# A streaming-encoder layer on one core: another issue order in the opening, residual rows loaded ahead, outputs finished in place, two divided weight units placed elsewhere

## The chip, the core and the metric

The kernel runs on one core of a Trainium2 chip. The metric is the device time of one execution in microseconds. The core has five engines that each work through their own instructions in order: TensorE (PE, matrix products and transposes; PEld is its weight load), VectorE (DVE), ScalarE (ACT), GpSimd (POOL) and SyncE (SP). Transfers between memory and the core's SBUF are issued by an engine and run on 16 DMA engines. Nearly all are issued by SP here, a few by POOL. An issue stands in its engine's order like any other instruction.

## The reference

The input is `x`, 2048 frames of 1024 float32 values. One layer is computed (DEPTH is 1):

```
h    = rmsnorm(x, norm_mix)
proj = h @ w_in                        # 1024 -> 2560 columns for four groups
y_a = short gated convolution          # columns cv_h, cv_b, cv_c
y_b = S5 state-space scan + GLU        # s5_u, with log_dt, lam, b, c, d
y_c = sliding-window attention         # a_q, a_k, a_v
y_d = HGRN2 gated linear recurrence    # hg_q, hg_f, hg_i, hg_g
y = rmsnorm of each group, concatenated
x = x + y @ w_out
h = rmsnorm(x, norm_ffn)
x = x + square(relu(h @ w_ff1)) @ w_ff2
```

## The kernel before

Frames lie in four blocks of 512 (`NB`, `TB`). Every matrix product is done in a split form: each float32 operand becomes a high and a low part, and a product takes three matmuls (hi·hi, lo·hi, hi·lo). At the clock's full level one 128x512 matmul follows the next every 0.23 us.

**The opening.** `make_hT(b)` loads the four 128-frame tiles of a block (`xt`, two buffers), squares each on ACT (L486), forms the mean on DVE (`rsx`, L92) and its power -1/2 on POOL (L93), scales on DVE with the gain row `g_mix` (L488), transposes on PE (L501), and copies the transposed halves out as `hh` (ACT, L505) and `hl` (DVE, L506). `attn_in` then multiplies tile by tile with the attention columns of `w_in`; `load_split` loads each weight tile `wr` through SP and splits it into `wh` (ACT, L105) and `wl` (DVE, L111). Behind it stand the HGRN columns, whose first matmul of the swapped kind is `mm<-hh,wh`. Some 15 small constants are loaded through POOL (`mraw` to `wgr`, L146 to L199), and then those of the S5 set-up (`lam`, `cn`, `bn`, `ldt`, `db`, L229 to L244). The two `ldt` loads are gathers of single 4-byte elements. A tile scheduler decides the order on each engine from the order of the program text and from priorities (`first`, `tc.high_priority`).

**The output projection.** `outp(b)` makes for each half `nh` of the columns four row tiles `i`; `ps` is the product in PSUM, `xr` the residual rows of `x` (two buffers), their sum goes to DRAM as `x1d`.

**The second feed-forward product.** It runs as seven groups `n` = 0 to 6 of eight row tiles `q` (a Strassen form); each tile is 16 units of three matmuls (L1548). `s_tile` loads and splits the moving side (`sr`, `st`), `t_unit` the weight units of the next group; `split2` puts the split units in turn into 26 slots. `X` and `Y` are running sums in SBUF. `finish` ends a row tile of the output:

```
r = tmp2(); SY.dma_start(out=r, in_=x1_d[...])
tsub(r, r, acc, ALU.add)        # acc is X or Y: tq<-tq,X
o = tmp2(); tsub(o, ps, r, ALU.add)   # tq<-mm,tq
SY.dma_start(out=a["out"][...], in_=o)
```

It is called for n = 1, 5 and twice for n = 6. `psum_mm` has two buffers, so a product that is not yet read holds back the one after the next.

Of the kernel before, what the change touches and what calls it, by code (L numbers as in the profile page):

```python
# [59 lines left out]
def emit(ctx, tc, a):  # L60
# [150 lines left out]
    def s5_setup():  # L211
        with tc.tile_pool(name="st", bufs=1) as st:
# [256 lines left out]
            for gp in range(8):  # L469
# [6 lines left out]
                yield  # L476


    def make_hT(b):

        def norm(i):
            t0 = b * TB + i * P
            xt = big.tile([P, D], F32, tag="xt", name="xt", bufs=2)
            SY.dma_start(out=xt, in_=a["x"][t0:t0 + P, :])
            ss = mix.tile([P, 1], F32, tag="ssx", name="ssx", bufs=2)
            S.activation(out=junk, in_=xt, func=AF.Square, accum_out=ss)  # L486
            r = rstd_of(mix, ss, 1, 1.0 / D, "rsx")
            V.scalar_tensor_tensor(out=xt, in0=xt, scalar=r, in1=g_mix, op0=ALU.mult, op1=ALU.mult)  # L488
            return xt

        nx = norm(0)
        yield
        for i in range(4):
            xt = nx
            if i < 3:
                nx = norm(i + 1)
            for k4 in range(2):
                pt = psum_tr()
                for k in range(4):
                    kk = k4 * 4 + k  # L500
                    PE.transpose(pt[:, k * P:(k + 1) * P], xt[:, kk * P:(kk + 1) * P], ident)  # L501
                pv = pt.rearrange("p (k t) -> p k t", k=4)
                oh = hh[:, k4 * 4:k4 * 4 + 4, i * P:(i + 1) * P]
                ol = hl[:, k4 * 4:k4 * 4 + 4, i * P:(i + 1) * P]
# [1088 lines left out]
```

## Time and profile before

| | |
|---|---|
| median of 3 runs | 2293.39 us (2293.31 to 2297.61) |
| profiled execution, its own time | 2296.33 us |
| its span, first to last instruction | 2294.5 us |
| mean granted clock | 0.992 |
| PE busy | 2205.3 us, 96% |
| DVE / ACT / POOL busy | 63% / 42% / 8% |
| DMA | 372.97 MB, mean 163 GB/s |

The span is what the trace shows; the execution's own time has 1.8 us around it. Times of instructions below count from the start of the span. In a row of the timeline stand start, duration, engine and line, operation, what it writes and reads, and in brackets how long the engine was idle just before and what it waited for.

### The profile page before, as it was taken

To read this page: it belongs to the slowest core of one execution; us is meant where nothing else is said; L and a number is where in the kernel's file an instruction comes from. 1 tells how busy PE (TensorE), PEld (TensorE's weight loads), DVE (VectorE), ACT (ScalarE), POOL (GpSimd) and SP (SyncE) were. 2 spreads that over 40 slices of the span, in tenths; PEclk is the share of its full clock that TensorE was granted. 3 is DMA by queue.
4 is the path that set the end of the run, shared out by engine and by line. 5 is a ranking of instruction groups with operands and counts; after the bars stand their busy time and mean duration, and the time that the engine had idled before them with its cause. 6 is when DMAs were issued, how large, how long until landed. Compare 5 with 4: busy or idle time off the path is not lost.

```text
span 2294.5 us, 32511 instructions
## 1 busy us (share of the span) xinstructions
PE 2205.3 (96%) x11460; PEld 1755.9 (77%) x11460; DVE 1449.5 (63%) x3044; ACT 961.3 (42%) x1914; POOL 194.4 (8%) x251
## 2 busy tenths in 40 slices
PE   4999999999999999999999999999999999999899
PEld 3777777777777787777788878888878877888787
DVE  4796796797679664596666676555534455465343
ACT  3444325324433433465565565555533223223121
POOL 3112212112211210000000000000000010000000
PEclk9999999999999999999999999999999999999999
DMA  6333334333443457646667575554655587475544
GB/s 174 97 89 94 98 98 138 109 105 100 139 116 104 129 195 232 196 153 202 195 196 210 151 235 156 152 148 147 201 165 195 181 293 233 146 248 175 190 165 152
DMA packets 391476, 372.97 MB, mean 163 GB/s; under 512 B 30656, under 2 KB 305184, under 8 KB 391312
## 3 DMA queue, kind: packets, MB, share of 16 engines
q1 hardware_dynamic: 388976, 365.05, 51.7%
q0 software_dynamic: 2336, 5.84, 1.0%
q8 instruction: 90, 1.47, 0.3%
q14 instruction: 74, 0.61, 0.1%
HBM read 265.97 MB, written 103.82 MB: 161 GB/s over the span
## 4 chain that ended last, share of the span: by engine, by line
PE 42%; DMA 6%; DVE 3%; ACT 1%; issue 1%; SPq 0%; DVEq 0%; ACTq 0%
PE mm L1548 19%; PE mm L1363 13%; PE hx L1363 7%; DMA wr<-in_w_ff_dram 5%; PE mx L1363 3%; DVE st L1520 1%; DMA tr<-tb 1%; DMA sr<-as 1%; DVE wr L1217 1%; DVE wl L1208 0%; ACT wh L1207 0%; ACT st L1519 0%; DMA tq<-x1d 0%; DVE tp L1217 0%; DVE tb L1327 0%
## 5 line engine op out<-in xcount | busy, mean ns | idle before, releaser
L1548 PE MATMUL mm<-wh,st 128*128 128x512 f32 x1728 | 549.2, 395 | 13.8 <-DVE tq L1217 6.1
L1548 PEld LDWEIGHTS mm<-wh,st 128*128 128x128 f32 x1728 | 325.8, 189 | 92.3 <-issue 9.6
L1548 PE MATMUL mm<-wl,st 128*128 128x512 f32 x864 | 341.1, 395 | 0.2 <-DVE wl L1208 0.2
L1363 PE MATMUL mm<-tb,wh 128*128 128x512 f32 x1024 | 323.8, 397 | 4.0 <-ACT tp L1369 1.9
L1519 ACT ACTIVATE st<-sr 128x1024 fp32r<-128x1024 f32 x112 | 115.4, 1054 | 343.6 <-PE mm L1548 244.2
L1363 PEld LDWEIGHTS mm<-tb,wh 128*128 128x128 f32 x1024 | 190.9, 189 | 53.7 <-ACT tp L1382 5.4
L510 PE MATMUL mm<-wh,hh 128*128 128x512 f32 x512 | 212.4, 415 | 0.7 <-ACT hh L505 0.7
L512 PE MATMUL mm<-wh,hl 128*128 128x512 f32 x512 | 205.9, 402 | 0.0
L105 ACT ACTIVATE wh<-wr 128x512 fp32r<-128x512 f32 x224 | 138.2, 629 | 158.6 <-PE mm L511 113.8
L511 PE MATMUL mm<-wl,hh 128*128 128x512 f32 x512 | 204.6, 400 | 0.0
L1363 PE MATMUL mm<-tb,wl 128*128 128x512 f32 x512 | 202.4, 396 | 1.0 <-DVE wl L1208 1.0
L1207 ACT ACTIVATE wh<-wr 128x512 fp32r<-128x512 f32 x204 | 124.8, 627 | 176.1 <-DVE wr L1217 83.4
L1548 PEld LDWEIGHTS mm<-wl,st 128*128 128x128 f32 x864 | 162.8, 188 | 38.9 <-DVE wl L1208 0.9
L1520 DVE TENSOR_TENSOR st<-sr,st 128x1024 fp32r<-128x1024 f32 x112 | 134.5, 1221 | 70.6 <-ACT st L1519 70.5
L111 DVE TENSOR_TENSOR wl<-wr,wh 128x512 fp32r<-128x512 f32 x224 | 150.2, 690 | 35.8 <-ACT wh L105 34.7
L1363 PE MATMUL hx<-tb,wh 128*128 128x512 f32 x512 | 161.1, 394 | 0.0
L1208 DVE TENSOR_TENSOR wl<-wr,wh 128x512 fp32r<-128x512 f32 x204 | 136.6, 687 | 36.5 <-ACT wh L1207 30.2
L510 PE MATMUL mm<-hh,wh 128*128 128x512 f32 x384 | 159.4, 415 | 0.0
L512 PE MATMUL mm<-hh,wl 128*128 128x512 f32 x384 | 152.7, 398 | 0.0
L511 PE MATMUL mm<-hl,wh 128*128 128x512 f32 x384 | 152.3, 397 | 0.0
L1363 PEld LDWEIGHTS mm<-tb,wl 128*128 128x128 f32 x512 | 96.6, 189 | 23.7 <-DVE wl L1208 1.4
L510 PEld LDWEIGHTS mm<-wh,hh 128*128 128x128 f32 x512 | 98.6, 193 | 20.8 <-ACT hh L505 1.3
(412 smaller groups left out, 3617.1 us busy)
## 6 DMA issues: line engine op xcount, KB each, us to landing
wr<-in_w_ff_dram SPq DMA_DIRECT2D x304, 256.0 KB, 3.9
as<-tp SPq DMA_DIRECT2D x224, 256.0 KB, 2.7
sr<-as SPq DMA_DIRECT2D x112, 512.0 KB, 4.6
wr<-in_w_in_dram SPq DMA_DIRECT2D x160, 256.0 KB, 3.1
wr<-in_w_out_dram SPq DMA_DIRECT2D x64, 256.0 KB, 4.0
xt<-in_x_dram SPq DMA_DIRECT2D x16, 512.0 KB, 3.6
xr<-in_x_dram SPq DMA_DIRECT2D x32, 256.0 KB, 3.0
x1d<-xr SPq DMA_DIRECT2D x32, 256.0 KB, 2.5
```

The source lines that it names most:

```text
L105: S.activation(out=hi, in_=raw, func=AF.Copy)
L111: (G if le == "p" else V).tensor_tensor(out=lo, in0=raw, in1=hi, op=ALU.subtract)
L510: PE.matmul(ps, lhsT=lh, rhs=rh, start=first, stop=False)
L511: PE.matmul(ps, lhsT=lh, rhs=rl, start=False, stop=False)
L512: PE.matmul(ps, lhsT=ll, rhs=rh, start=False, stop=last)
L1207: S.activation(out=h, in_=raw, func=AF.Copy)
L1208: V.tensor_tensor(out=l, in0=raw, in1=h, op=ALU.subtract)
L1217: V.tensor_tensor(out=o, in0=x, in1=y, op=op)
L1363: PE.matmul(ps, lhsT=(wh, wl)[lw][:, ks], rhs=b[lb][:, k, :], start=first and k == 0 and q == 0, stop=k == 3 and q == 2, skip_group_check= ...
L1519: S.activation(out=s_[:, 0, ks], in_=r, func=AF.Copy)
L1520: V.tensor_tensor(out=s_[:, 1, ks], in0=r, in1=s_[:, 0, ks], op=ALU.subtract)
L1548: PE.matmul(ps, lhsT=st_[:, ls, k, :], rhs=tu[n, k][lt], start=k == 0 and p_ == 0, stop=k == NJ - 1 and p_ == 2)
```

## The change

1. `make_hT` and its first run stand ahead of the constants in the program text. All constants are issued behind the first power on POOL (`tc.issue_after(norms[0][0])`), the loads of the S5 set-up behind the fourth, and the first part of block 0's `attn_in` behind the first scaling. `issue_after` orders instructions that are on the same engine; it adds no wait between engines.
2. `outp` issues the load of `xr` ahead of the row tile's matmuls, with high priority.
3. In the second feed-forward product `ahead(n, q)` loads the residual rows and adds X or Y to them in the turn of the tile before; `finish(ps, rs)` then adds `ps` in place and stores.
4. In `split2` the 10th and 11th unit go to the slots in pool `c1` ("xr", "gain"), which were the 25th and 26th; the others keep the slots in `t2p`.

```diff
-        G.tensor_tensor(out=r, in0=r, in1=mhalf[:, 0:n], op=ALU.pow)
+        pows.append(G.tensor_tensor(out=r, in0=r, in1=mhalf[:, 0:n], op=ALU.pow).ins)
...
+    with first(-4000):
+        run(make_hT(0))
+    after = tc.issue_after(norms[0][0])
+    after.__enter__()
     masks = cm.tile([P, 4, P], U8, name="masks")
     mraw = mix.tile([P, 4, P], F32, tag="cva0", name="mraw")
     G.dma_start(out=mraw, in_=a["c_masks"])
...
+    after.__exit__(None, None, None)
...
-                ps = yield from tm_tile(ws, i)
                 xr = c1.tile([P, 512], F32, tag="xr", name="xr", bufs=2)
                 t0 = b * TB + i * P
-                SY.dma_start(out=xr, in_=a["x"][t0:t0 + P, ns])
+                with tc.high_priority():
+                    SY.dma_start(out=xr, in_=a["x"][t0:t0 + P, ns])
+                ps = yield from tm_tile(ws, i)
...
-    next(setup)
+    with tc.issue_after(norms[3][0]):
+        next(setup)
     for b in range(NB):
-        dense(attn_in(b))
+        g = attn_in(b)
+        if b == 0:
+            with tc.issue_after(norms[0][1]):
+                next(g)
+        dense(g)
...
-        if n < NW + NB2:
+        if n == NW:
+            return split(raw, c1, ("xr", "xr"), 2)
+        if n > NW + 1:
             return split(raw, t2p, ("vh", "vl"), NB2)
-        if n == NW + NB2:
-            return split(raw, c1, ("xr", "xr"), 2)
...
+    ENDS = {1: (("X", 0, 0),), 5: (("X", 1, 0),), 6: (("X", 1, 1), ("Y", 0, 1))}
+    def ahead(n, q):
+        t0, rs = (q % 4) * P, []
+        for acc, tb, nd in ENDS.get(n, ()):
+            b_ = (q // 4) * 2 + tb
+            r = tmp2()
+            SY.dma_start(out=r, in_=x1_d[b_][t0:t0 + P, nd * 512:(nd + 1) * 512])
+            tsub(r, r, (X if acc == "X" else Y)[:, q], ALU.add)
+            rs.append((r, a["out"][b_ * TB + t0:b_ * TB + t0 + P, nd * 512:(nd + 1) * 512]))
+        return rs
+    def finish(ps, rs):
+        for r, dst in rs:
+            tsub(r, ps, r, ALU.add)
+            SY.dma_start(out=dst, in_=r)
...
             if (n, q) != (6, 7):
                 s_next = s_tile(*((n, q + 1) if q < 7 else (n + 1, 0)))
+                r_next = ahead(*((n, q + 1) if q < 7 else (n + 1, 0)))
...
-            elif n == 5:
-                finish(q, ps, X[:, q], 1, 0)
-            else:
-                finish(q, ps, X[:, q], 1, 1)
-                finish(q, ps, Y[:, q], 0, 1)
+            finish(ps, ends)
```

The first place where instructions move is the opening, on DVE and on POOL. On DVE, of before, from its first conversion to the first `hl`:

```order
L147 CAST masks<-mraw 128x512
L92 TENSOR_SCALAR rsx<-ssx 128x1
L111 TENSOR_TENSOR wl<-wr,wh 128x512 x7
L488 SCALAR_TENSOR_TENSOR xt<-xt,rsx,g_mix 128x1024
L111 TENSOR_TENSOR wl<-wr,wh 128x512
```

The same stretch of the changed kernel, whose line numbers differ:

```order
L94 TENSOR_SCALAR rsx<-ssx 128x1
L168 SCALAR_TENSOR_TENSOR xt<-xt,rsx,g_mix 128x1024
L94 TENSOR_SCALAR rsx<-ssx 128x1
L113 TENSOR_TENSOR wl<-wr,wh 128x512 x2
L168 SCALAR_TENSOR_TENSOR xt<-xt,rsx,g_mix 128x1024
L187 TENSOR_TENSOR hl<-tr,hh 128x4x128
L113 TENSOR_TENSOR wl<-wr,wh 128x512 x3
```

The scaling of the first tile stood behind the mask conversion and seven weight splits, and stands behind none now. Further on in DVE's order is the first operation that reads `ldt`, of before with the fourth `hl` of the opening's eight ahead of it:

```order
L506 TENSOR_TENSOR hl<-tr,hh 128x4x128
L742 COPY va<-mm 128x128
L223 TENSOR_SCALAR t_783<-ldt 128x8
L217 TENSOR_TENSOR db<-db,ident 16x256
L766 TENSOR_REDUCE qss<-qsq 128x6
```

and of the changed kernel, with all eight `hl` ahead of it:

```order
L187 TENSOR_TENSOR hl<-tr,hh 128x4x128
L793 TENSOR_TENSOR qn<-qk,qrs 128x128
L168 SCALAR_TENSOR_TENSOR xt<-xt,rsx,g_mix 128x1024
L273 TENSOR_SCALAR t_783<-ldt 128x8
L267 TENSOR_TENSOR db<-db,ident 16x256
L271 TENSOR_SCALAR t_784<-t_783 128x8
L271 TENSOR_SCALAR t_784<-t_784 128x8
L761 COPY va<-mm 128x128
```

The operation on `ldt` now stands behind the whole of the opening's own work on DVE and ahead of the copy `va<-mm` of a later `attn_in` tile.

On POOL, of before, the loads up to the first power (`rsx<-rsx,mhalf`):

```order
L146 DMA mraw<-in_c_masks_dram 128x512
L149 DMA bones<-in_c_bones_dram 128x2
L154 DMA g_grp<-in_group_norm_dram 128x768
L156 DMA g_grpa<-in_group_norm_dram 128x2x1
L159 DMA convw<-in_conv_w_dram 128x3x1 x2
L165 DMA qgain<-in_attn_q_norm_dram 64x1 x2
L165 DMA kgain<-in_attn_k_norm_dram 64x1 x2
L168 DMA sink<-in_attn_sinks_dram 64x2x1
L93 ISA
L93 TENSOR_TENSOR rsx<-rsx,mhalf 128x1
```

and of the changed kernel, its first six rows of work:

```order
L95 ISA
L95 TENSOR_TENSOR rsx<-rsx,mhalf 128x1
L198 DMA mraw<-in_c_masks_dram 128x512
L201 DMA bones<-in_c_bones_dram 128x2
L203 DMA g_grp<-in_group_norm_dram 128x768
L95 TENSOR_TENSOR rsx<-rsx,mhalf 128x1
```

The first power stood behind eleven loads and stands ahead of all now. The S5 set-up loads, which stood behind the second power, come later in the changed kernel, behind the third and fourth:

```order
L223 DMA ogain<-in_hg_out_norm_dram 128x64
L226 DMA lbp<-in_hg_lower_bounds_dram 128x2x1
L248 DMA wgr<-in_s_w_glu_dram 128x512 x2
L95 TENSOR_TENSOR rsx<-rsx,mhalf 128x1 x2
L279 DMA lam<-in_s_lam_re_dram 8x128
L280 DMA lam<-in_s_lam_im_dram 8x128
```

The eleven set-up loads follow one another from `lam` on, with `ldt` and `db` last, as they did.

The second place is SP in the output projection of block 1, where its second half of columns begins (`x1d<-xr` is the store of a finished row tile, `ybt` the loads of the next stage). Of before:

```order
L1109 DMA xr<-in_x_dram 128x512
L1112 DMA x1d_64<-xr 128x512
L102 DMA wr<-in_w_out_dram 128x512 x8
L1112 DMA x1d_64<-xr 128x512
L1109 DMA xr<-in_x_dram 128x512 x2
L1112 DMA x1d_64<-xr 128x512
```

and of the changed kernel:

```order
L1128 DMA xr<-in_x_dram 128x512
L1132 DMA x1d_64<-xr 128x512
L104 DMA wr<-in_w_out_dram 128x512 x3
L1128 DMA xr<-in_x_dram 128x512
L104 DMA wr<-in_w_out_dram 128x512 x5
L1132 DMA x1d_64<-xr 128x512 x2
L1128 DMA xr<-in_x_dram 128x512 x2
```

The `xr` load of the half's first row tile stood behind all eight weight loads and a store, and stands behind three weight loads.

The third place is DVE where group n = 5 begins. Of before, up to the first output tile of that group:

```order
L1208 TENSOR_TENSOR wl<-wr,wh 128x512
L1217 TENSOR_TENSOR wr<-wr 128x512 x3
L1520 TENSOR_TENSOR st<-sr,st 128x1024
L1217 TENSOR_TENSOR wr<-wr 128x512
L1520 TENSOR_TENSOR st<-sr,st 128x1024
L1217 TENSOR_TENSOR wr<-wr 128x512
L1217 TENSOR_TENSOR tq<-tq,X 128x512
L1217 TENSOR_TENSOR tq<-mm,tq 128x512
```

and of the changed kernel up to its second:

```order
L1225 TENSOR_TENSOR wl<-wr,wh 128x512
L1234 TENSOR_TENSOR wr<-wr 128x512 x2
L1234 TENSOR_TENSOR tq<-mm,tq 128x512
L1537 TENSOR_TENSOR st<-sr,st 128x1024
L1234 TENSOR_TENSOR wr<-wr 128x512 x2
L1537 TENSOR_TENSOR st<-sr,st 128x1024
L1234 TENSOR_TENSOR wr<-wr 128x512
L1234 TENSOR_TENSOR tq<-mm,tq 128x512
```

The first add that reads the product (`tq<-mm,tq`) stood behind two `st`, two `wr` and the add of X to loaded rows; it stands ahead of them, and the add of X is no longer beside it.

## Rows read from the trace of the kernel before

**Rows 1.** The page's busy time by engine (share of the span, instructions).

```profile
PE 2205.3 (96%) x11460; PEld 1755.9 (77%) x11460; DVE 1449.5 (63%) x3044; ACT 961.3 (42%) x1914; POOL 194.4 (8%) x251
```

**Rows 2.** The waits of PE, the longest sums: what waits, for whom, microseconds in total, how often, the longest.

```profile
PE tr L501 <- DVE xt L488: 21.9, 1, 21.9
PE tr L501 <- DVE hl L506: 8.5, 3, 7.6
PE tr L1093 <- DVE hl L1098: 6.8, 4, 3.0
PE mm L1548 <- DVE tq L1217: 6.1, 1, 6.1
```

**Rows 3.** The timeline of the opening up to PE's first transpose (all engines, rows picked).

```profile
3.72 1.52 POOL L159 DMA_DIRECT2D convw<-in_conv_w_dram  x2
4.32 1.06 ACT L486 ACTIVATE junk<-xt 128x1024 bf16<-128x1024 f32 x1 [2.30 <-DMA xt<-in_x_dram]
7.37 0.43 DVE L147 CAST masks<-mraw 128x512 uint8<-128x512 f32 x1 [5.76 <-DMA mraw<-in_c_masks_dram]
7.71 0.15 DVE L92 TENSOR_SCALAR rsx<-ssx 128x1 f32<-128x1 f32 x1
11.33 0.59 POOL L93 TENSOR_TENSOR rsx<-rsx,mhalf 128x1 f32<-128x1 f32 x1
20.56 1.28 DVE L488 SCALAR_TENSOR_TENSOR xt<-xt,rsx,g_mix 128x1024 f32<-128x1024 f32 x1
21.89 0.47 PE L501 MATMUL tr<-ident,xt 128*128 128x128 f32 x1 [21.89 <-DVE xt L488]
```

**Rows 4.** The DMA issues of the first 60 us: how many, size of one, median microseconds from issue to landing.

```profile
wr<-in_w_in_dram SPq DMA_DIRECT2D x15, 256.0 KB, 4.5
xt<-in_x_dram SPq DMA_DIRECT2D x6, 512.0 KB, 3.6
g_mix<-in_norm_mix_dram SPq DMA_DIRECT2D x1, 512.0 KB, 7.7
...
ldt<-in_s_log_dt_dram POOLq DMA_DIRECT2D x2, 2.0 KB, 10.4
```

**Rows 5.** The timeline from the set-up loads to the first HGRN matmul with swapped operands (rows picked; L741 reads the first `attn_in` tile's product).

```profile
24.07 0.55 POOL L229 DMA_DIRECT2D lam<-in_s_lam_re_dram  x1
...
25.11 1.50 POOL L234 DMA_DIRECT2D cn<-in_s_c_re_dram  x2
...
33.53 0.49 ACT L741 ACTIVATE qk<-mm 128x384 f32<-128x384 f32 x1 [0.79 <-PE mm L512]
...
42.71 0.17 DVE L223 TENSOR_SCALAR t<-ldt 128x8 f32<-128x8 f32 x1 [7.81 <-DMA ldt<-in_s_log_dt_dram]
...
44.66 0.47 PE L501 MATMUL tr<-ident,xt 128*128 128x128 f32 x1 [7.62 <-DVE hl L506]
...
61.80 0.39 PE L510 MATMUL mm<-hh,wh 128*128 128x512 f32 x1
```

**Rows 6.** Stretches of the span: length, busy time of PE, PEld, DVE, ACT, POOL with the instructions of each, granted clock of PE, DMA share, GB/s.

```profile
22.00:28.00 6.00, 4.73 (x14) 3.32 (x15) 4.25 (x12) 2.08 (x6) 5.34 (x8) 1.00 0.85 240
44.60:48.60 4.00, 3.94 (x12) 3.27 (x13) 2.74 (x8) 1.09 (x3) 1.29 (x2) 0.50 0.41 123
931.50:936.00 4.50, 4.50 (x15) 3.62 (x16) 0.90 (x3) 0.49 (x1) 0.00 (x0) 0.63 0.61 204
2142.50:2147.90 5.40, 5.38 (x13) 4.29 (x14) 3.44 (x4) 0.00 (x0) 0.00 (x0) 0.51 0.68 213
1640.00:1645.00 5.00, 5.00 (x23) 4.08 (x22) 1.98 (x3) 2.50 (x5) 0.00 (x0) 1.00 0.26 73
```

**Rows 7.** The timeline of the output projection at two places.

```profile
876.93 0.42 SPq L1109 DMA_DIRECT2D xr<-in_x_dram  x1
...
881.53 0.69 DVE L1111 TENSOR_TENSOR xr<-mm,xr 128x512 f32<-128x512 f32 x1 [5.15 <-DMA xr<-in_x_dram]
882.75 0.33 PE L1093 MATMUL tr<-ident,ybt 128*128 128x128 f32 x1 [2.98 <-DVE hl L1098]
...
931.50 0.33 PE L1093 MATMUL tr<-ident,ybt 128*128 128x128 f32 x1 [2.00 <-DVE hl L1098]
```

**Rows 8.** The timeline at the start of the second feed-forward product.

```profile
1666.47 1.26 ACT L1207 ACTIVATE wh<-wr 128x512 fp32r<-128x512 f32 x2 [7.61 <-DMA wr<-in_w_ff_dram]
1667.15 0.50 PE L1548 MATMUL mm<-wh,st 128*128 128x512 f32 x1 [2.26 <-ACT wh L1207]
```

**Rows 9.** The timeline at the first output tile of group n = 5.

```profile
2135.73 0.42 SPq L1529 DMA_DIRECT2D tq<-x1d  x1
...
2138.46 0.69 DVE L1217 TENSOR_TENSOR wr<-wr 128x512 f32<-128x512 f32 x1 [3.13 <-DMA wr<-in_w_ff_dram]
...
2140.96 0.69 DVE L1217 TENSOR_TENSOR tq<-tq,X 128x512 f32<-128x512 f32 x1 [1.81 <-DMA tq<-x1d]
2141.68 0.69 DVE L1217 TENSOR_TENSOR tq<-mm,tq 128x512 f32<-128x512 f32 x1
2142.52 0.77 PE L1548 MATMUL mm<-wh,st 128*128 128x512 f32 x1 [6.08 <-DVE tq L1217]
```

**Rows 10.** The timeline of DVE behind the last product.

```profile
2289.89 0.68 DVE L1217 TENSOR_TENSOR tq<-tq,Y 128x512 f32<-128x512 f32 x1
...
2290.60 0.69 DVE L1217 TENSOR_TENSOR tq<-mm,tq 128x512 f32<-128x512 f32 x1
```

More of the change, by code (lines that the diff above doesn't have):

```diff
@@ L87, in emit @@
     V.memset(ones, 1.0)
+    pows = []
     def rstd_of(pool, ss, n, inv, tag):
@@ L143, in emit, with run, make_hT, norm @@
     junks = {k: cm.tile([P, GW], BF16, name="junk" + k) for k in "chg"}
+    g_mix = c1.tile([P, D], F32, tag="gain", name="g_mix")
+    with first(-3998):
+        SY.dma_start(out=g_mix, in_=a["norm_mix"].partition_broadcast(P))
+    def run(g):
+        r = None
+        for r in g:
+            pass
+        return r
+    norms = []
+    def make_hT(b):
+        def norm(i):
+            t0 = b * TB + i * P
+            xt = big.tile([P, D], F32, tag="xt", name="xt", bufs=2)
+            SY.dma_start(out=xt, in_=a["x"][t0:t0 + P, :])
+            ss = mix.tile([P, 1], F32, tag="ssx", name="ssx", bufs=2)
+            S.activation(out=junk, in_=xt, func=AF.Square, accum_out=ss)
+            r = rstd_of(mix, ss, 1, 1.0 / D, "rsx")
+            i_ = V.scalar_tensor_tensor(out=xt, in0=xt, scalar=r, in1=g_mix, op0=ALU.mult, op1=ALU.mult)
+            norms.append((pows[-1], i_.ins))
+            return xt
+        nx = norm(0)
+        yield
+        for i in range(4):
+            xt = nx
+            if i < 3:
+                nx = norm(i + 1)
+            for k4 in range(2):
+                pt = psum_tr()
+                for k in range(4):
+                    kk = k4 * 4 + k
+                    PE.transpose(pt[:, k * P:(k + 1) * P], xt[:, kk * P:(kk + 1) * P], ident)
+                pv = pt.rearrange("p (k t) -> p k t", k=4)
+                oh = hh[:, k4 * 4:k4 * 4 + 4, i * P:(i + 1) * P]
+                ol = hl[:, k4 * 4:k4 * 4 + 4, i * P:(i + 1) * P]
+                S.activation(out=oh, in_=pv, func=AF.Copy)
+                V.tensor_tensor(out=ol, in0=pv, in1=oh, op=ALU.subtract)
+                yield
+    with first(-4000):
+        run(make_hT(0))
+    after = tc.issue_after(norms[0][0])
+    after.__enter__()
     masks = cm.tile([P, 4, P], U8, name="masks")
@@ L149, in emit @@
     G.dma_start(out=bones, in_=a["c_bones"])
-    g_mix = c1.tile([P, D], F32, tag="gain", name="g_mix")
-    with first(-3998):
-        SY.dma_start(out=g_mix, in_=a["norm_mix"].partition_broadcast(P))
     g_grp = cm.tile([P, 3 * GW], F32, name="g_grp")
@@ L475, in s5_setup @@
                 SY.dma_start(out=two_d[:, gp, 2:4, :], in_=wsb)
[L476 to L504, printed above, removed]
-                S.activation(out=oh, in_=pv, func=AF.Copy)
-                V.tensor_tensor(out=ol, in0=pv, in1=oh, op=ALU.subtract)
                 yield
@@ L1113, in outp @@
                 yield True
-    def run(g):
-        r = None
-        for r in g:
-            pass
-        return r
     tracks = []
@@ L1148, in dense @@
             advance()
-    with first(-4000):
-        run(make_hT(0))
     s5p = None
     setup = s5_setup()
-    next(setup)
+    with tc.issue_after(norms[3][0]):
+        next(setup)
     for b in range(NB):
-        dense(attn_in(b))
+        g = attn_in(b)
[3 more added lines that the diff above has]
+        dense(g)
         drain("hg")
@@ L1524, in emit @@
     Y = t2p.tile([P, 8, 512], F32, name="Y")
[L1526 to L1533 removed]
+    ENDS = {1: (("X", 0, 0),), 5: (("X", 1, 0),), 6: (("X", 1, 1), ("Y", 0, 1))}
[12 more added lines that the diff above has]
+            SY.dma_start(out=dst, in_=r)
     tu = {(0, k): t_unit(0, k) for k in range(NJ)}
[L1536 removed]
+    s_next, r_next = s_tile(0, 0), []
     for n in range(7):
@@ L1539, in emit @@
             st_ = s_next
+            ends = r_next
             if (n, q) != (6, 7):
                 s_next = s_tile(*((n, q + 1) if q < 7 else (n + 1, 0)))
+                r_next = ahead(*((n, q + 1) if q < 7 else (n + 1, 0)))
             if n < 6 and q >= 3:
```

11 lines of the change are left out of this document (removed).

## The prediction

> **What bounds the kernel now.** I read the busy times first: PE works 96% of the span [rows 1]. No edit takes a matmul or a transpose away, so all that can be won lies in the other 4% and in stretches at a lower clock. The second view is the list of PE's waits [rows 2]. It is headed by three waits that belong to the lines of the diff: 21.9 us before the first transpose, 8.5 us for `hl` of the opening, of which one is 7.6, and 6.1 us for a `tq` add in the second feed-forward product. The timeline around each then says what is late [rows 3, 5, 7, 8, 9], and the table of stretches says what the clock did behind the longer ones [rows 6].
>
> At the start the first `x` tile is there at 4.32 us, since ACT squares it then, but DVE makes its mean only at 7.71, behind the mask conversion that waits for a POOL load, POOL forms the power at 11.33 behind its loads, and DVE scales at 20.56 behind seven weight splits; PE begins at 21.89 [rows 3]. At 37 us PE stands again, for 7.62 us: DVE waits at the operation on `ldt` until 42.71, and the fourth `hl` is queued behind it [rows 5]. That operation needs the `ldt` load, whose first neighbour was issued at 24.07.
>
> **The change part by part: the opening.** Now the mean, the power and the scaling of the first tile stand behind no load and no split. Square from 4.32 for 1.06, mean 0.15, power 0.59 [rows 3]: about 6.3 us with the hand-overs. The scaling also needs the gain row, issued within the first 2 us, which took 7.7 us in a start crowded by POOL's loads [rows 4]: it begins between 7 and 9.5 and takes 1.28 [rows 3], so PE transposes from about 10 instead of 21.89. The weights don't come 12 us earlier, though. Their issue stood where it stands, they took 4.5 us in the median [rows 4], ACT still waits for one at 21.43 by the weights' own queue, and PE worked 4.73 of 6 us from 22 to 28 at half pace, 14 instructions [rows 6]. I let the first `attn_in` tile end at 24 instead of 33.53 [rows 5]; that is 9.5 of the 11.9 us kept.
>
> From 33.53 to the first swapped HGRN matmul at 61.80 are 28.27 us [rows 5]. Without the idle 7.62 and the half of 4.0 us that the clock at 0.50 cost [rows 6], 18.65 us of work are left. Loads of `x` tiles (3.6 us, [rows 4]) and norms now follow each other more closely behind an earlier PE; I add 3.6 for one such wait and get 24 + 18.65 + 3.6 = 46.3 us for the place that was at 61.80. This is the upper bound of the gain, 15.5 us.
>
> It will not be reached, because the wait for `ldt` moves rather than goes. The set-up loads stand behind the fourth power. The fourth `x` tile gets a buffer when the second has been transposed, near 25; plus 3.6 to land, 1.06, 0.15 and 0.59 with hand-overs is 31.4 us. In before the operation on `ldt` ran 42.71 - 24.07 = 18.64 us after the first set-up issue [rows 5], so now it runs at 50. On DVE the `db` product, two small operations and then the copy `va` of a later tile are queued behind it; that copy frees a product bank, so PE resumes at about 51. It would have stood 51 - 46.3 = 4.7 us, and the half-clock stretch behind such an idle cost 2.0 us before [rows 6]; I take 2.5. The gain is 61.80 - 51 - 2.5 = 8.3; I take 8, with bounds 3 (the loads take a quarter longer) and 15.5.
>
> **The constants behind the first power.** Sixteen POOL issues come later by about 5 us. First to be read are the masks, on DVE, now behind the third `hl`, which can't be there before the second tile's transposes near 18; their load is the first behind the power at 6.3, and with the 7.7 us of the slow gain row [rows 4] it would land at 14 to 15. I cost this at nothing; without that cover DVE would stand before `hl` of the second tile, at most the 5 us by which they are late, which is inside the bound of 3.
>
> A row on POOL bears on all its loads: two issues took 1.52 us while DVE was idle (at 3.72, [rows 3]) and two took 1.50 at 25.11 [rows 5] in a stretch where DVE was busy 4.25 of 6 us [rows 6]. The Trainium skill ("SBUF — State Buffer", section "SBUF: two separate sides") says the opposite: a DMA issued from GpSimd can't write its descriptors while VectorE holds the port pair they share, and one of 620 ns alone took 3100 ns beside a VectorE copy. By that page eleven set-up issues beside a DVE that is busier now would bring `ldt` some 27 us later and the opening would lose 19 us instead of winning 8. The two rows here don't show such stretching.
>
> **Output projection.** PE stands 2.98 us before 882.75 and 2.00 before 931.50, behind the sum of `xr`, which on DVE waited more than 5 us for its load; the load was issued at 876.93, after the product [rows 7]. In 931.5 to 936.0 the clock was 0.63, which cost 4.5 x 0.37 = 1.67 [rows 6]. The load now stands behind three weight loads of the half instead of all eight and a store, some 4 us ahead. Sum 2.98 + 2.00 + 1.67 = 6.65. Two bounds: 3, if the loads of the following tiles, of which two buffers are all there are, are late by as much at one of the two places, and 6.7. I take 6, as the load of the second tile is ahead by little.
>
> **Early slots.** The start of the second feed-forward product stood 2.26 us for a weight split; ACT had waited 7.61 us for the load [rows 8]. With two units more that have a slot of their own before the tail of the stage ahead is through, two more can be loaded early, and from 1640 to 1645 the DMA engines were busy by 0.26 [rows 6], so there is room. Taken: 2.5, with a short wait of the same kind behind it; bounds 0 and 3.5. What is late if it fails is the third unit, no worse than now.
>
> **Residual rows ahead in the second product.** At the first output tile of group 5 the load of `x1d` was issued at 2135.73, after the product of the tile, DVE waited for it until 2140.96, and the add at 2141.68 freed the bank; PE stood 6.08 us until 2142.52 [rows 9]. Behind it 5.40 us ran at clock 0.51 [rows 6], 5.40 x 0.49 = 2.65 us. Both go if the bank is read as soon as the product ends: 8.7. In the changed order the add that reads the product needs no load, and stands ahead of the weight difference that waited 3.13 us for its load at 2138.46 [rows 9]. That wait remains on DVE, a little later, and the weights of the group after are the next thing that can be late: bounds 5 and 9.5.
>
> The adds in place are as many as before (0.69 each), one load and one store for each tile are the same; only which buffer they use and when differs. At the end the addition of Y, 2289.89 to 2290.60 between the last two adds [rows 10], is done ahead: 0.6.
>
> **Sum.** 8 + 6 + 2.5 + 8.7 + 0.6 = 25.8 us. The profiled span of 2294.5 would become 2268.7; the profiled execution took 2296.33, 2.9 above the median of 2293.39, and the gains are differences, so I subtract from the median: 2267.6.
>
> **The rivals.** (A) *The opening's stall is only moved, all of it.* If the set-up loads take a quarter longer (18.64 becomes 23), or the fourth power is later than 31.4, PE resumes at 56 or later and G = 0 to 3. For it: they run beside the third and fourth `x` tile and the weight loads. Time 2293.4 - (17.8 + 1.5) = 2274. Chance 0.17.
>
> (B) *The opening clears completely.* If `ldt` is ready by 46, for instance because the loads meet fewer others, the gain there is 15.5, the time 2293.4 - 33.3 = 2260. Against it: 10.4 us from issue to landing for `ldt` [rows 4], the longest of the list. Chance 0.17.
>
> (C) *The stall of group 5 becomes another.* DVE's weight difference waits 3.13 us for its load [rows 9]; if the weight loads or the `sr` tiles are what ends last there, PE stands for `st` instead. Gain there 0 to 3, time 2293.4 - (25.8 - 8.7 + 1.5) = 2275. Chance 0.12.
>
> (D) *The change does not do what it says*: the scheduler's other moves eat the earlier start, and the loads ahead meet others; only the tail and one stall go, 4 us or less, time 2290 to 2293. Against it: the orders show each load moved. Chance 0.05.
>
> (E) *POOL starves and the layer is slower.* If DVE, which is busy earlier now, slows POOL's issue of the eleven set-up loads, every late microsecond of `ldt` is one of PE. The whole sum is 25.8 us, so `ldt` must come that much later than I forecast to break even, 2.3 us more for each issue; slower by 0.2% needs 2.8. At 4 us more an issue, 44 us in all, the time would be 2293.4 + 44 - 25.8 = 2311.6. Against it: the two pairs of issues above, 1.52 and 1.50. This is the case that the page of the Trainium skill on the SBUF speaks for. Chance 0.04. Another 0.05 is for joint cases of A, C and D.
>
> **How the numbers follow.** The forecast, all five terms within their bounds, has 0.40, at 2267.6 with a range of 2262 to 2273 of its own; A, B and C hold 0.46. About 0.2% (4.6 us) is what a measurement of this kernel can tell from no change. All of the forecast, A, B, C (0.86) and most joint cases (0.04) lie beyond it: faster 0.90; within it lie D and the other joint cases: 0.06; slower is E: 0.04. The range takes in A, B and C with some microseconds beside them and leaves out D, E and part of the joint cases: 2256 to 2283.
>
> **What would show it.** PE's first transpose near 10 us and the first `mm<-hh,wh` near 53 with one wait of some 5 us for a DVE copy ahead of it; right before that DVE waiting for `ldt` near 50. No wait of PE above 1 us near 883 and 931 of before's places, nor at the first tile of group 5; the `tq` add right behind its product. The clock near 1.00 behind those places. The forecast is wrong if PE waits over 8 us in the opening, if a wait for `st` or `wh` over 3 us appears in group 5, or if the `xr` sums still wait for their loads.

## The result: 2275.6 us, 0.85% faster, where 2267.6 was forecast

The changed kernel takes 2275.59 us (median of 4 executions, 2274.96 to 2276.07) where the kernel before, executed beside it, takes 2294.63. The ratio is 0.9915, with a 95% interval of 0.9900 to 0.9931. The forecast of a faster kernel holds, and so does the range of 2256 to 2283, but 19.0 us are won and not 25.8, and the narrower range that the forecast gave for its own case, 2262 to 2273, does not hold. The two profiled spans are 2294.5 and 2273.4 us, 21.1 apart.

The page of the changed kernel begins with these rows of busy time by engine, which answer to [rows 1]:

```profile
span 2273.4 us, 32514 instructions
PE 2201.7 (97%) x11460; PEld 1753.2 (77%) x11460; DVE 1445.5 (64%) x3044; ACT 960.2 (42%) x1914; POOL 192.7 (8%) x251
```

Its longest waits of PE (what waits, for whom, microseconds in total, times, longest) answer to [rows 2]:

```profile
PE tr L182 <- DVE xt L168: 9.9, 1, 9.9
PE mm L529 <- DVE va L761: 4.8, 1, 4.8
PE tr L182 <- DVE hl L187: 4.4, 1, 4.4
PE hx L1054 <- DVE hy L1070: 4.3, 5, 2.3
PE mm L1576 <- DVE Y L1234: 4.2, 2, 2.5
PE tr L1112 <- DVE hl L1117: 3.6, 5, 1.5
...
PE mm L529 <- ACT hh L186: 2.9, 1, 2.9
...
PE mm L1576 <- ACT X L1579: 2.4, 1, 2.4
```

The wait before the first transpose fell from 21.9 to 9.9 us. The wait of 7.6 for `hl` is gone, and in the opening one of 4.8 for the copy `va`, one of 4.4 for `hl` and one of 2.9 for `hh` are new. The 6.1 for a `tq` add is gone. Two waits for `Y`, 4.2 together (1.8 before), stand in the second product, and one of 2.4 for the copy of a product to `X` (1.0 before).

Both kernels run 11460 matmuls and transposes on PE, nearly all in the same order, so the start of the matmul with the same number can be compared between the traces. This table is worked out from the starts in the traces. "Idle" is PE's idle time within the stretch. "Clock" is half of the time in which PE worked at the lower level, which is what the lower level cost there. The first microseconds of PE's work are counted in it: 128x512 matmuls start every 0.43 us there instead of every 0.23, although the granted clock of that stretch reads 1.00 ([rows 6], 22 to 28). Without them the last line is 14.8, 19.9, 10.1 and 17.3. A second profiled execution of each kernel stands beside the first.

| stretch (matmul numbers) | before | again | after | again | first pair, won |
|---|---|---|---|---|---|
| start to 0 | 21.9 | 20.4 | 9.9 | 10.1 | 12.0 |
| 0 to 128: opening | 39.9 | 41.0 | 42.6 | 41.1 | -2.7 |
| 128 to 1800: projections, mixers | 268.9 | 272.2 | 272.0 | 274.5 | -3.1 |
| 1800 to 5300 | 511.7 | 514.2 | 511.8 | 513.8 | 0.0 |
| 5300 to 5800: output projection, blocks 1 and 2 | 115.1 | 113.9 | 111.1 | 109.0 | 4.0 |
| 5800 to 8800: rest of it, first product | 696.6 | 695.3 | 695.7 | 698.4 | 1.0 |
| 8800 to 9200: second product begins | 96.9 | 95.0 | 94.7 | 94.6 | 2.2 |
| 9200 to 10100: groups 1 and 2 | 214.8 | 214.2 | 216.4 | 215.7 | -1.6 |
| 10100 to 10800 | 162.2 | 162.2 | 162.2 | 162.2 | -0.1 |
| 10800 to 11000: group 5 begins | 55.1 | 55.7 | 46.1 | 46.1 | 9.0 |
| 11000 to last start | 105.8 | 105.8 | 106.1 | 106.1 | -0.2 |
| behind the last start | 5.6 | 5.6 | 5.0 | 5.0 | 0.7 |
| idle, 0 to the last | 61.8 | 59.1 | 56.6 | 54.0 | 5.2 |
| clock | 17.3 | 23.2 | 12.9 | 19.9 | 4.4 |

The timeline of the changed kernel's opening (rows picked) shows both halves of what the forecast expected there:

```profile
8.52 1.28 DVE L168 SCALAR_TENSOR_TENSOR xt<-xt,rsx,g_mix 128x1024 f32<-128x1024 f32 x1 [2.65 <-DMA g_mix<-in_norm_mix_dram]
9.86 0.47 PE L182 MATMUL tr<-ident,xt 128*128 128x128 f32 x1 [9.86 <-DVE xt L168]
...
26.73 0.16 DVE L228 TENSOR_TENSOR lbm<-lbp 128x2 f32<-128x2 f32 x1 [3.29 <-DMA lbp<-in_hg_lower_bounds_dram]
28.75 0.47 PE L182 MATMUL tr<-ident,xt 128*128 128x128 f32 x1 [4.41 <-DVE hl L187]
...
33.41 0.58 POOL L279 DMA_DIRECT2D lam<-in_s_lam_re_dram  x1
39.12 1.38 POOL L290 DMA_DIRECT2D ldt<-in_s_log_dt_dram  x2
...
51.44 0.17 DVE L273 TENSOR_SCALAR t<-ldt 128x8 f32<-128x8 f32 x1 [6.56 <-DMA ldt<-in_s_log_dt_dram]
52.14 0.28 DVE L761 COPY va<-mm 128x128 f32<-128x128 f32 x1
52.48 0.64 PE L529 MATMUL mm<-hh,wh 128*128 128x512 f32 x1 [4.80 <-DVE va L761]
```

The scaling waits for the gain row alone and PE begins at 9.86. The set-up loads start at 33.41, `ldt` is there at 51.44, 18.0 us later, DVE reaches `va` behind it, and PE stands 4.80 us until 52.48. That matmul stood at 61.80 [rows 5].

At group 5 and at the end, the timeline shows the adds that [rows 9] and [rows 10] showed:

```profile
2118.11 0.68 DVE L1234 TENSOR_TENSOR tq<-mm,tq 128x512 f32<-128x512 f32 x1
...
2268.85 1.29 DVE L1234 TENSOR_TENSOR tq<-mm,tq 128x512 f32<-128x512 f32 x2 [9.80 <-PE mm L1576]
```

The add stands 6.4 us ahead of the place where PE needs its bank (matmul 10836 starts at 2124.55), PE has no idle time there, and the last two adds follow each other. Counted in tiles of 48 matmuls from the end, the tile that PE waited to begin in [rows 9] is the fourth of group 5, so the add that freed its bank is that of the second tile; the forecast called it the first.

### The profile page after: what moved, and what is told of

It reads as the page before. It is cut to its first block, busy times and chain, and to the rows that moved or that the text cites. A ratio compares the mean times of both kernels' runs of the same rounds, so it can differ in the third digit from the quotient of the medians.

```text
span 2273.4 us, 32514 instructions
## 1 busy us (share of the span) xinstructions
PE 2201.7 (97%) x11460; PEld 1753.2 (77%) x11460; DVE 1445.5 (64%) x3044; ACT 960.2 (42%) x1914; POOL 192.7 (8%) x251
## 4 chain that ended last, share of the span: by engine, by line
issue 31%; PE 20%; DMA 1%; DVE 1%; POOL 0%; ACT 0%; SPq 0%; DVEq 0%; POOLq 0%; ACTq 0%
PE mm L1576 17%; PE mm L1380 2%; PE hx L1380 1%; DMA wr<-in_w_ff_dram 0%; DMA fxs<-x1d 0%; DVE tp L1234 0%; POOL tt L1523 0%; PE mx L1380 0%; DMA tt<-wr 0%; ACT wh L1224 0%; SPq L1329 0%; DVE wl L1225 0%; POOL frs L95 0%; PE tr L1281 0%; PE sx L1281 0%
## 5 line engine op out<-in xcount | busy, mean ns | idle before, releaser
L107 ACT ACTIVATE wh<-wr 128x512 fp32r<-128x512 f32 x224 | 137.5, 628 | 162.9 <-PE mm L530 111.1
L1380 PEld LDWEIGHTS mm<-tb,wl 128*128 128x128 f32 x512 | 96.1, 188 | 24.3 <-DVE wl L1225 2.1
```

Source lines behind the costliest of these rows:

```text
L107: S.activation(out=hi, in_=raw, func=AF.Copy)
L1380: PE.matmul(ps, lhsT=(wh, wl)[lw][:, ks], rhs=b[lb][:, k, :], start=first and k == 0 and q == 0, stop=k == 3 and q == 2, skip_group_check= ...
```

## The experiments

Executions of one and the same kernel lie up to 14 us apart here (before: 2288.9 to 2302.6 over all jobs), so each experiment is read in two ways: by its ratio to the kernel before, timed in the same job, and by the stretches of its one profile.

**Both kernels once more.** No edit.

> The kernel before, once more with a profile. If the forecast's terms were sized from stalls that belong to the kernel, the waits of 7.6, 3.0, 2.0 and 6.1 us are there again within 0.5 us each, and 115 us lie between the 5300th and the 5800th matmul. If a part of them is chance, they differ here by 1 us or more, and the term of the output projection (6 us) is the one to suspect: the changed kernel with its loads as before needed 111.5 us for that stretch.

> The changed kernel once more, timed beside the three that follow, so that they have a neighbour on the same chip. Both theories of the result: 2274 to 2278 here, ratio to before 0.990 to 0.993. If its profile has as many half-clock stretches as the first one had, the stretches belong to the kernel; if their number and places differ at the same waits, they are chance and the 21 us between the two first profiles hold a part of chance.

The changed kernel took 2279.01 us here (2274.29 to 2281.39), ratio 0.9929 (0.9914 to 0.9945); before took 2297.31 in the one execution. The waits of PE of the kernel before, in the second profile:

```profile
PE tr L501 <- DVE xt L488: 20.4, 1, 20.4
PE tr L501 <- DVE hl L506: 8.5, 3, 7.6
PE mm L1548 <- DVE tq L1217: 7.4, 1, 7.4
PE tr L1093 <- DVE hl L1098: 5.8, 4, 3.0
```

and three rows of its timeline, at the places of [rows 7]:

```profile
888.19 0.61 PE L1093 MATMUL tr<-ident,ybt 128*128 128x128 f32 x3 [3.03 <-DVE hl L1098]
...
936.24 0.69 DVE L1111 TENSOR_TENSOR xr<-mm,xr 128x512 f32<-128x512 f32 x1 [5.90 <-DMA xr<-in_x_dram]
...
937.46 0.55 PE L1093 MATMUL tr<-ident,ybt 128*128 128x128 f32 x3 [0.92 <-DVE hl L1098]
```

The waits of 7.6 and 3.0 are there again, that of 6.1 is 7.4. The wait of 2.00 is 0.92, although DVE waited longer for the load (5.90 against 5.20 us). The wait of 2.26 us for a weight split at the start of the second product [rows 8] is not there at all. A third profile with this order, that of the kernel before with `log_dt` loaded as rows (below), has 3.86 and 1.21 us at the two places of [rows 7] and no wait for a weight split either. So the stall of the opening and that of group 5 belong to the kernel; the wait for a weight split and part of the second gap of the output projection, on which two terms of the forecast rested, are not there in every execution.

The lower clock level is a second thing that one execution shows by chance. PE waited 1.32 us for the same S5 step in the first profile of before and 1.33 in that of the changed kernel, in these two rows:

```profile
301.66 1.04 PE L445 MATMUL sx<-E,bb 64*16 64x128 f32 x8 [1.32 <-DVE H L447]
```

```profile
293.82 1.04 PE L495 MATMUL sx<-E,bb 64*16 64x128 f32 x8 [1.33 <-DVE H L497]
```

The stretches around them (length, busy times, then granted clock, DMA share, GB/s), of before and of after:

```profile
300.30:305.00 4.70, 3.38 (x19) 2.65 (x19) 4.70 (x12) 0.96 (x3) 0.00 (x0) 1.00 0.11 35
```

```profile
295.00:298.60 3.60, 3.60 (x10) 2.78 (x10) 2.88 (x7) 1.26 (x2) 0.00 (x0) 0.53 0.00 0
```

The clock stayed at 1.00 in one and was 0.53 in the other. In the second profile of before it fell there, too. The sum of what the lower level cost was 17.3 and 23.2 us in the two profiles of before and 12.9 and 19.9 in those of after. Of the 21.1 us between the first spans 4.4 are this difference.

**The opening as before.** The edits of the output projection, of `finish` and of the slots alone, on the kernel before:

```diff
-    with first(-4000):
-        run(make_hT(0))
-    after = tc.issue_after(norms[0][0])
-    after.__enter__()
...
-    with tc.issue_after(norms[3][0]):
-        next(setup)
+    next(setup)
...
-            with tc.issue_after(norms[0][1]):
-                next(g)
```

> Parts 2 to 4 of the change without the opening. The first HGRN matmul with swapped operands came 9.3 us earlier in the changed kernel and the lead had shrunk to 6.2 us by the 1800th matmul. Theory (the opening is worth what is left of the lead): 6 to 8 us slower than the changed kernel, 2282 to 2284, with the 7.6 us wait for hl and the stall at ldt back. Rival (the lead would be taken back later anyway, since another transfer is late at the same time): under 3 us slower, 2276 to 2279.

2288.30 us (2284.01 to 2289.88), ratio 0.9956 (0.9937 to 0.9974). Against 0.9922, the mean of the two ratios of the whole change (0.9915 and 0.9929), the opening is worth 0.0034 of 2295 us, 7.8 us. That is the size that the theory named, give or take the 4 us of this ratio's interval; the time itself lies above the 2282 to 2284 expected, in a job in which the kernel before, too, took more (2297.10). The waits are back: 21.7 before the first transpose and 7.2 for `hl`.

**The output projection as before.**

```diff
-                with tc.high_priority():
-                    SY.dma_start(out=xr, in_=a["x"][t0:t0 + P, ns])
                 ps = yield from tm_tile(ws, i)
+                xr = c1.tile([P, 512], F32, tag="xr", name="xr", bufs=2)
+                SY.dma_start(out=xr, in_=a["x"][t0:t0 + P, ns])
```

> The changed kernel with the residual loads of the output projection issued behind each product, as before. Theory (the forecast's term of 6 is mis-sized because the early loads hold weight loads back): 2 to 4 us slower, 2278 to 2280; the waits near 875 and 923 come back with 3.0 and 2.0 us and the ones near 844 and 894 get shorter. Rival (the forecast's term is right and something else ate the gain): 5 to 7 us slower, 2281 to 2283.

2280.89 us (2277.12 to 2288.38), ratio 0.9934 (0.9912 to 0.9955). That is 2.8 us above the mean of the two ratios of the whole change, with intervals that overlap. The longest wait behind `hl` in the output projection is 2.1 us; its second place shows in the timeline as

```profile
927.40 0.69 DVE L1130 TENSOR_TENSOR xr<-mm,xr 128x512 f32<-128x512 f32 x1 [5.35 <-DMA xr<-in_x_dram]
...
928.61 0.55 PE L1112 MATMUL tr<-ident,ybt 128*128 128x128 f32 x3 [0.44 <-DVE hl L1117]
```

DVE waits as long for its load as in before, 5.35 us, and PE waits 0.44 for it instead of 2.00. The order on each engine in this stage is that of before. The stretch from matmul 5300 to 5800 took 111.5 us here, against 115.1 and 113.9 in before.

**The finish as before.**

```diff
-                r_next = ahead(*((n, q + 1) if q < 7 else (n + 1, 0)))
...
+            elif n == 5:
+                finish(q, ps, X[:, q], 1, 0)
```

> The changed kernel with the output finished as before: residual rows loaded at the tile's own turn, a second buffer for the sum; the early slots stay. Theory: the stall at the first tile of group 5 with its half-clock stretch (8.9 us) and the 0.6 us of the tail come back, and what the early loads cost at the start of the second product (some 1 to 2 us) goes: 7 to 9 us slower, 2283 to 2285. Rival (the early loads of group 1 also cause the longer waits in group 2): 4 to 6 us slower, 2280 to 2282.

2286.57 us (2281.44 to 2290.77), ratio 0.9955 (0.9937 to 0.9973). By the ratios the part is worth 0.0033, 7.6 us. The timeline at group 5 has the stall of before:

```profile
2124.19 0.42 SPq L1547 DMA_DIRECT2D tq<-x1d  x1
2125.72 0.69 DVE L1234 TENSOR_TENSOR tq<-tq,X 128x512 f32<-128x512 f32 x1 [1.94 <-DMA tq<-x1d]
2126.45 0.69 DVE L1234 TENSOR_TENSOR tq<-mm,tq 128x512 f32<-128x512 f32 x1
...
2127.29 0.76 PE L1566 MATMUL mm<-wh,st 128*128 128x512 f32 x1 [7.07 <-DVE tq L1234]
```

The stretch of group 5 took 56.2 us, 10.1 more than in the changed kernel, and groups 1 and 2 took 213.7, 2 to 3 less. The stall is back, as the theory said. What the early loads cost is given back in groups 1 and 2, not at the start of the second product, where the theory had it: that stretch took 96.1 us, against 94.7 and 94.6.

**The slots as before.**

```diff
-        if n == NW:
-            return split(raw, c1, ("xr", "xr"), 2)
-        if n > NW + 1:
+        if n < NW + NB2:
             return split(raw, t2p, ("vh", "vl"), NB2)
+        if n == NW + NB2:
+            return split(raw, c1, ("xr", "xr"), 2)
```

> The changed kernel with the 10th and 11th divided unit in the t2p slots again. Theory: the 2.3 us wait for a weight split at the start of the second product comes back, 2 to 3 us slower, 2277.5 to 2278.5. Rival (the start is held by the DMA engines, not by slots): within 1 us, 2275 to 2276.5.

2275.04 us (2272.93 to 2276.22), ratio 0.9903 (0.9885 to 0.9921): no worse than the whole change. The start of the second product took 97.1 us instead of 94.7 in the profile, with the wait of 2.2 us for `wh` back, but the sum does not show it. Over all profiles this stretch took 94.5 to 97.3 us with the early slots (nine) and 95.0 to 97.1 without (five), so the slots do not set it.

**`log_dt` loaded as rows.** One load of 16 contiguous values to each partition and two small copies in place of the two gathers:

```diff
-            for g2 in range(2):
-                G.dma_start(out=ldt[g2 * 64:(g2 + 1) * 64, :],
-                             in_=a["s5_log_dt"].rearrange("(q g) -> g q", g=2)[g2].partition_broadcast(64),
-                             allow_slow_non_contiguous=True)
+            ldr = small("ldr", 16)
+            G.dma_start(out=ldr, in_=a["s5_log_dt"].partition_broadcast(P))
...
+            for g2 in range(2):
+                V.tensor_copy(out=ldt[g2 * 64:(g2 + 1) * 64, :],
+                              in_=ldr.rearrange("p (q g) -> p g q", g=2)[g2 * 64:(g2 + 1) * 64, g2, :])
```

> The changed kernel with log_dt loaded as one row of 16 values to all partitions, and two small copies on DVE that pick every second value, in place of two gathers of single 4-byte elements. Theory (the opening's remaining 4.8 us stall is the wait for these gathers): ldt is there near 43 instead of 51.3, the wait of PE before the first swapped HGRN matmul goes or is under 1 us, the half-clock stretch behind it too, and the time falls by 5 to 7 us, to 2269 to 2271. Rival (any of the eleven set-up loads would be as late, since they are issued at 33 to 41 us and share the engines with others): PE still waits 3 us or more, the time falls by less than 2 us.

2268.73 us (2268.06 to 2269.67), ratio 0.9888 (0.9871 to 0.9905). The timeline of the place:

```profile
38.08 0.56 POOL L290 DMA_DIRECT2D ldr<-in_s_log_dt_dram  x1
43.20 0.34 DVE L295 COPY ldt<-ldr 64x8 f32<-64x8 f32 x2 [1.32 <-DMA ldr<-in_s_log_dt_dram]
...
45.66 0.28 DVE L762 COPY va<-mm 128x128 f32<-128x128 f32 x1
...
46.37 0.39 PE L530 MATMUL mm<-hh,wh 128*128 128x512 f32 x1
```

The row is there 5 us after its issue, the gathers needed 12.3 (39.12 to 51.44). PE's wait before the first swapped matmul is gone; it starts at 46.37 instead of 52.48. The theory holds, and this is the fastest version here, 10.3 us below the changed kernel in the same job (the profiled spans are 6.7 and 9.9 apart) and 25.6 below the kernel before. The load of `db`, issued behind that of `log_dt`, landed 4.7 us after its issue, where it took 11.0 behind the gathers.

The same edit on the kernel before:

> The kernel before with log_dt loaded as rows, nothing else changed. Theory (in before too the gathers of single elements are what DVE waits for until 42.7): the wait of 7.6 us is under 2 us, and the time falls by 6 to 9 us, to 2286 to 2288 where before is at 2294.5. Rival (the fourth hl would wait anyway, for the x tile that landed at 43.9): under 3 us.

2288.29 us (2282.23 to 2292.60) beside 2295.71, ratio 0.9964 (0.9952 to 0.9976): 7.4 us from one load. The wait of 7.6 us is 2.1, where under 2 was expected:

```profile
PE tr L502 <- DVE hl L507: 3.7, 3, 2.1
```

**The early load for one tile only.**

```diff
+                if nh == 1 and i == 0:
+                    with tc.high_priority():
+                        xr = load_xr()
                 ps = yield from tm_tile(ws, i)
+                if not (nh == 1 and i == 0):
+                    xr = load_xr()
```

> The changed kernel with the residual load ahead of the product for the first row tile of the second column half only; the other loads behind the products as before. Theory (that one load is what the stall needed; the other early loads stand ahead of weight loads and cost about what they bring): the stretch from the 5300th to the 5800th matmul takes 1 to 3 us less than the 111.1 of the changed kernel, time 1 to 3 us less. Rival (the early loads of the following tiles are needed too): 1 to 4 us more.

2277.98 us (2271.00 to 2281.24), ratio 0.9921 (0.9902 to 0.9940). The stretch took 109.5 us, less than the 111.1 of the first profile and more than the 109.0 of the second. This does not tell the two apart.

**The residual rows of group 1 at their own turn.**

```diff
-                r_next = ahead(*((n, q + 1) if q < 7 else (n + 1, 0)))
+                nn, qq = (n, q + 1) if q < 7 else (n + 1, 0)
+                r_next = [] if nn == 1 else ahead(nn, qq)
...
+            elif n == 1:
+                ends = ahead(n, q)
```

> The changed kernel with the residual rows of group 1 loaded at the tile's own turn; groups 5 and 6 stay ahead. Theory (the eight loads of 256 KB issued from 1647 to 1676 cost the start of the second product, and the order that they force costs group 2): the stretch from matmul 8800 to 10100 takes 2 to 3 us less than the 311.1 of the changed kernel and the time falls by 2 to 3 us. Rival (the longer waits in groups 0 and 2 come from PE being earlier, with the same loads behind them): within 1 us.

2276.68 us (2271.65 to 2281.30), ratio 0.9923 (0.9906 to 0.9940). Matmuls 8800 to 10100 took 314.9 us, not less than 311.1. The theory that the early loads of group 1 cost groups 0 to 2 falls.

**Two parts taken back on the kernel with `log_dt` as rows.** The edits are the one to `log_dt` and, first, that of "the output projection as before", then that of "the slots as before".

> The changed kernel with log_dt as rows, and the output projection's residual loads behind the products as before. Beside the 2268.7 of the same kernel with the early loads: theory (the early loads are worth 1 to 3 us, not the 6 forecast): 2270 to 2272. Rival of the forecast: 2274 to 2276. Rival that they are worth nothing: 2268 to 2269.5.

2273.41 us (2268.76 to 2273.88), ratio 0.9897 (0.9882 to 0.9912). The time lies between the two bands expected; by the ratio, beside 0.9888, it is 2.1 us, the theory's size, but that lies within the intervals, so no difference at all is not ruled out. The stretch from 5300 to 5800 took 111.2 us, as with the early loads (111.1).

> The changed kernel with log_dt as rows, and the 10th and 11th divided unit in the t2p slots as before. Beside 2268.7: theory (the early slots are worth the 2.2 us wait that they remove at the start of the second product): 2270.5 to 2271.5. Rival (the wait only moves to a later unit or to the reader of the product): within 1 us, 2268 to 2270.

2270.18 us (2265.09 to 2276.96), ratio 0.9889 (0.9871 to 0.9907), the same as with the early slots. That is the rival's number; a difference of 2 us would still lie within the intervals.

## Why the prediction was right, and where its sizes were off

**The opening (8 forecast) was right in size and in mechanism.** First transpose at 9.9 for "about 10"; set-up loads from 33.4 for 31.4; `ldt` 18.0 us later for 18.6; PE resuming at 52.5 for 51, after 4.8 us idle for 4.7. The stretch behind the stall ran at a lower clock, as forecast:

```profile
52.50:56.50 4.00, 4.00 (x11) 3.17 (x12) 3.41 (x12) 0.00 (x0) 0.55 (x1) 0.57 0.07 16
```

That costs 1.7 us. At matmul 260 the changed kernel was 7.6 us ahead and at 1600 still 7.8; at 1800 it was 6.2, because the clock fell once more behind the 1.33 us wait shown above. Two steps of the working met by luck: the constants, costed at nothing, did make PE wait 4.41 us, since `lbp` was there only at 26.73, 8.8 us after its issue (5.0 in before); this took the place of the 3.6 us that had been added for a late `x` tile. The upper bound, 46.3 us for the first swapped matmul without a wait for `ldt`, is what the kernel with `log_dt` as rows shows, 46.37, with the same 4.4 us for `hl` in it. PE's waits between the first transpose and the first swapped matmul grew from 9.2 to 12.1 us in all. The forecast's sign of being wrong, over 8 us of waiting in the opening, is met if the sum is meant and not if a single wait is (4.8).

**Group 5 (8.7) and the tail (0.6) were right**: 9.0 and 0.7 in the first pair, and 10.1 us when the finish was put back. Over all profiles the stretch at group 5 took 46.1 to 46.3 us with the new finish (ten) and 55.1 to 56.2 with the old (four).

**The output projection (6) is the term that failed in its size**: 4.0 in the first pair, and by the ratios 2 to 3 for the part alone. The step that failed was to add up the three gaps of one execution, 2.98 + 2.00 + 1.67, as what the late loads cost. With the same order on every engine the stretch took 115.1, 113.9 and 115.7 us in the kernel before (twice, and with `log_dt` as rows) and 111.5 and 111.2 in the changed kernel with its loads as before (without and with the rows). The second gap was 2.00, 0.92, 1.21, 0.44 and 0.64 us, while DVE waited 4.7 to 5.9 us for the load each time; the first was 2.98, 3.03, 3.86, 2.12 and 2.19. So of this stretch 2.4 to 4.5 us stayed away when the late loads were put back into the changed kernel, although the order here is that of before; why stays open. With the early loads it took 108.2 to 111.1 us (eight profiles), which leaves 0 to 3 us to the loads themselves. In the changed kernel the load of the first tile helps less than reckoned, too: it stands between weight loads and landed 6.5 us after its issue at 866.53, so that DVE still waited 2.40 us (the trace names a weight load that landed with it), and the next tile's add waits for its own load.

```profile
873.12 0.69 DVE L1131 TENSOR_TENSOR xr<-mm,xr 128x512 f32<-128x512 f32 x1 [2.40 <-DMA wr<-in_w_out_dram]
...
879.92 0.69 DVE L1131 TENSOR_TENSOR xr<-mm,xr 128x512 f32<-128x512 f32 x1 [3.93 <-DMA xr<-in_x_dram]
```

That is the case of the low bound of 3 in the forecast, "late by as much at one of the two places", against which it took 6. One of its signs of being wrong is met: `xr` sums still wait for their loads, though PE's waits at the two places are under 1 us.

**The early slots (2.5) were sized from a wait that a second execution of before does not have.** The stretch is 2.2 us shorter in the first pair, 0.4 in the second, and taking the slots back changed no time that can be measured. The lower bound of 0 is what the runs bear out. In place of the wait for a weight split PE now waits 2.39 us in the same stretch for ACT to copy a finished product:

```profile
1660.53 1.06 ACT L1579 ACTIVATE X<-mm 128x512 f32<-128x512 f32 x2
1661.16 0.50 PE L1576 MATMUL mm<-wh,st 128*128 128x512 f32 x1 [2.39 <-ACT X L1579]
```

This wait is 2.1 to 3.4 us in all nine profiles with the early slots and 1.0 to 1.4 in all five without.

**Not forecast: 1.6 us given back in groups 1 and 2.** PE waits there for the add into `Y` (4.2 us against 1.8), which on DVE is queued behind weight differences that wait for their loads:

```profile
1887.99 0.69 DVE L1234 TENSOR_TENSOR wr<-wr 128x512 f32<-128x512 f32 x1 [2.90 <-DMA wr<-in_w_ff_dram]
1888.60 0.68 DVE L1234 TENSOR_TENSOR Y<-mm,X 128x512 f32<-128x512 f32 x1
...
1889.43 0.76 PE L1576 MATMUL mm<-wh,st 128*128 128x512 f32 x1 [2.55 <-DVE Y L1234]
```

The waits for `st` became shorter there, from 2.4 to 0.7 us, so that PE's idle time grew by 0.4 us only (4.5 to 4.9; 4.3 to 4.4 in the second pair). The other 1.5 us are the lower clock level behind the wait for `Y`, which before did not have in this stretch:

```profile
1889.40:1893.00 3.60, 3.57 (x9) 2.57 (x10) 2.75 (x3) 0.00 (x0) 0.12 (x1) 0.57 0.72 222
```

With the finish as before PE was idle for 2.6 us, the lower level cost 1.7, and the stretch took 213.7. That the loads of group 1 are the cause of the longer waits for `Y` was tried and fell; which part of the new order is, stays open.

**The sum.** Of the forecast's 25.8 us the first pair of profiles has 21.1: 2.0 are missing in the output projection, 1.8 in the opening, where 6.2 us are left at matmul 1800, 1.6 in groups 1 and 2, 0.3 at the slots, and 1.0 came by itself in the first product. The medians have 19.0 and, in the second job, 15.3 us; the clock's share of a pair changes by several microseconds from execution to execution, which the forecast did not take in, though its range held it.

**The rivals.** A (the stall moved whole) would have needed PE to resume at 56; it resumed at 52.5. B (it clears) did not come from this change but from loading `log_dt` as rows. Against B the forecast called the 10.4 us of `ldt` the longest landing of its list; `db`, issued behind `ldt`, took 11.7 in before. C did not come: PE has no idle time at group 5. D, 4 us or less, did not come with 19.0. E, POOL starving, did not come, and the rows show no trace of it: beside a DVE that was busy 3.10 of 7.60 us two pairs of the set-up issues took

```profile
34.47 1.49 POOL L284 DMA_DIRECT2D cn<-in_s_c_re_dram  x2
35.95 1.42 POOL L284 DMA_DIRECT2D cn<-in_s_c_im_dram  x2
```

and the stretch of all eleven (length, busy times of PE, PEld, DVE, ACT and POOL, clock, DMA share, GB/s) is

```profile
33.40:41.00 7.60, 7.60 (x39) 6.19 (x38) 3.10 (x6) 3.36 (x6) 7.60 (x12) 1.00 0.83 197
```

That is 7.6 us for eleven issues, 0.69 each, and 1.49 and 1.42 for the pairs, as in before (1.50, [rows 5]). The rule of the Trainium skill ("SBUF — State Buffer", section "SBUF: two separate sides") that GpSimd can't write its descriptors while VectorE runs an operation in a two-port mode does not show in these rows; whether DVE's operations here are of that kind no run here shows.

## What to carry to other kernels

Look at what a moved stall waits for before moving the work around it: here two gathers of 4-byte elements were worth 7 to 10 us, as much as the reordering of the whole opening, and the reordering could not get past them. Size a term from a stall only when a second execution has it too; where an engine's own wait stays the same, PE's idle time behind it still varied by 1 to 2 us here. And what is won at one place by loading ahead has to be set against what stands behind those loads in the same queue.

## What the runs showed of the hardware beyond that

The granted clock fell behind some waits of PE and not behind others of the same length at the same instruction: behind the 1.33 us in the changed kernel and not behind the 1.32 in before, behind the 3.03 us at 888.19 in the second profile of before and not behind the 2.98 at 882.75 in the first. Where it fell, PE ran at 1.2 instead of 2.4 GHz for some microseconds. In the profiled executions of these kernels the lower level cost 12.9 to 27.5 us in all, as the table counts it, a spread of 14.6 us beside the 21.1 between the first spans. The gathers of `log_dt` kept the DMA engines busy while they moved next to nothing: from 36 to 52 us, in 40 slices, busy tenths and GB/s are

```profile
DMA  8967463773962699995000005099990000000000
GB/s 328 406 259 263 138 208 77 90 82 41 154 72 51 236 420 349 145 33 21 0 0 0 0 0 0 0 1 1 1 2 0 0 0 3 3 10 5 21 0 0
```

with slices at 9 tenths busy and 1 to 2 GB/s late in the stretch. The trace holds 32 packets of 128 bytes there, 32 elements each; one took 3.3 us on average, while the packets of 1024 bytes of `db` behind them took 0.05.
